# Norm scales of two FFN mixers: two f32r products with a matrix of ones, refined on all partitions, in place of column means and turns

## The chip, the cores and the metric

The kernel runs on one core of a Trainium2 chip. TensorE (PE) multiplies out of SBUF into PSUM, VectorE (DVE), ScalarE (ACT) and GpSimd (POOL) work elementwise, and SP, ACT and POOL issue the DMAs. The metric is the device time of one execution in microseconds, the median of several runs.

## The reference

Two layers of a decoder on 1,024 tokens of 1,024 features. Each layer is a token mixer (layer 0 a gated short convolution, layer 1 banded attention) and a SwiGLU channel mixer with 2,816 hidden features, all with a norm ahead and a residual behind. What is computed at the place of the change is the norm ahead of each channel mixer:

```python
def rmsnorm(x, gain):
    r = lax.rsqrt(jnp.mean(x * x, axis=-1, keepdims=True) + EPS)   # one number for each token
    return (x * r) * gain

x = x + mix                              # mix ends in a product: ... @ w_out (or w_o)
h = rmsnorm(x, norm_ffn[i])
x = x + (silu(g) * u) @ w_down           # g, u = halves of h @ w_gate_up
```

## The kernel before

**Layout.** Activations lie transposed: features on partitions, tokens along a row. `X[m]` (m from 0 to 7) holds 128 features of all 1,024 tokens in f32. Products are made at f32 precision out of f32r parts: every operand is split into a high part (ACT casts it, L881) and a low part (DVE subtracts, L882), and a product is three steps of PE, high by high, high by low, low by high (L1061 to L1063 in the token mixer's output product, L946 to L948 elsewhere), each of 128x128 weights by 512 tokens.

**Order.** Nothing is scheduled by a tool there. A `Line` keeps a time axis in planned microseconds: `line.work` appends work of PE and moves `line.end` on by 0.2265 for each product; `at(t, f)` puts an instruction of another engine at a planned time. Run in order of time, this gives the order in which each engine gets its instructions; an engine then works them in that order, and waits where one is not ready. The planned times are no waits themselves.

**The place.** `channel_mixer` runs once for each layer. First come the eight output tiles of the token mixer's last product for tokens 0 to 511 (half 0), then eight for the other half; `begin1` and `begin2` are the planned ends of the two halves. Behind each tile DVE adds it to the residual (L1087), ACT squares it (L1085), DVE adds the squares (L1091) and POOL stores the residual (L1089). So `state["ss", h]` holds, on 128 partitions, partial sums of squares of each token; what is missing is the sum over partitions, and the result is wanted on all partitions, since `scale` (L1126) multiplies `X[m]` by it in place.

`half_chain(h, t)` makes it, once for each half of each layer, so four times in the kernel. `mean` puts four products on PE, 128 tokens of sums as weights and a column of ones as the moving operand (L1104), which turn the tokens onto partitions: 128x4 sums in PSUM bank P3. These products are f32 and not f32r, and each appears in the trace as two passes. `guess` forms the mean on DVE (L1109) and the inverse root: Ln and Exp on ACT (L263, L264) and one step of Newton on DVE (L265 to L268), all of 128x4. `turn` brings the result back with four transposes of a column that is broadcast to 128 columns (L1116): 128x512 scales in bank P2, equal on all partitions.

**What follows.** The gate-up product is made in one level of Strassen's scheme: seven kinds of products, k = 0 to 6, for four units first, 48 steps of PE for each kind, straight behind `begin2`. Its moving operands are sums of quarters of the scaled X: kind 0 and 1 use half 0 alone (even and odd tiles); kind 2 uses a sum T2 of all four quarters (L1190, L1196), made in four pieces, p = 0 to 3, each split by `put`; kinds 3 to 6 use more such sums (L1200, L1204). So half 0's scales are wanted 192 steps after half 0's last tile, and half 1's 96 steps after its own.

In layer 0 (`whole`) the weight sums for the first four units are also formed in the stretch of half 1's output products (`sums_in_place`, L874), stored to HBM by POOL (L877), and read back later.

Of the kernel before, what the change touches and what calls it, by code (L numbers as in the profile page):

```python
# [44 lines left out]
C_ROOM = 496  # L45
# [25 lines left out]
def trunk_kernel(ctx: ExitStack, tc: tile.TileContext, xT, small, table, w_in, w_out, w_kv, w_q, w_o, w_gu, w_dn, out):  # L71
# [146 lines left out]
    cst = slot("cst", (P, C_ROOM))[:, 0:C_END]  # L218
# [70 lines left out]
    def token_r_rows():  # L289

        ss = state["ss"]
        one = slot("s0", (P, P), F32R)
        dve.memset(plain(one), 1.0)
        hi, lo = slot("G3", dtype=F32R), slot("G4", dtype=F32R)
        m, t, rb = slot("G2"), slot("G5"), slot("G0")
        for h in range(2):
            c = slice(h * 512, h * 512 + 512)
            act.copy(hi[:, c], ss[:, c])
            dve.tensor_tensor(lo[:, c], ss[:, c], plain(hi)[:, c], ALU.subtract)
            ps = bank(("P2", "P3")[h])  # L300
            pe.matmul(ps, one, hi[:, c], start=True, stop=False)
            pe.matmul(ps, one, lo[:, c], start=False, stop=True)
            dve.tensor_scalar(m[:, c], ps, 1.0 / D, EPS, ALU.mult, ALU.add)
            act.activation(t[:, c], m[:, c], AF.Ln)
            act.activation(rb[:, c], t[:, c], AF.Exp, scale=-0.5)
            dve.tensor_tensor(t[:, c], rb[:, c], rb[:, c], ALU.mult)
            dve.scalar_tensor_tensor(t[:, c], t[:, c], -0.5, m[:, c], ALU.mult, ALU.mult)
            dve.scalar_tensor_tensor(rb[:, c], t[:, c], 1.5, rb[:, c], ALU.add, ALU.mult)
        return rb
# [17 lines left out]
    def conv_layer():  # L327
# [33 lines left out]
        for k in range(NK):  # L361
            if 0 < k < NK - 1:
                load_x(k + 1)
                if k % 2:
                    load_parts(k + 1, 2)
            if k == 4:
                nc.sync.dma_start(cst[:, C_SINK:], small[:, C_SINK:])
# [337 lines left out]
        t = group_end  # L705
        back("b0", "G10", t + 40.0)
# [298 lines left out]
    def channel_mixer(layer, next_stage, src_of, operands, raw_tags, extra_tags, slots, line, lead_in):  # L1005
# [12 lines left out]
        def tail_weights(h, m, t):  # L1018
# [18 lines left out]
            if layer == 1:  # L1037
                at(t - 13.0, load_parts)
            else:
                at(t - 14.0, load)  # L1040
                at(t - 5.2, hi)
                at(t - 4.2, lambda: it["steps"][1]())
# [53 lines left out]
        def half_chain(h, t):  # L1096

            v = {}

            def mean():  # L1100
                v["ps"] = bank("P3")
                ss = state["ss", h]
                for b in range(4):
                    pe.matmul(v["ps"][:, b : b + 1], ss[:, b * P : (b + 1) * P], ones, start=True, stop=True)  # L1104

            def guess():
                v["m"] = slot("hr_m", (P, NB, 2), bufs=2)[:, 0:4, 0]
                v["r"] = slot("hr_t", (P, NB, 2), bufs=2)[:, 0:4, 0]
                dve.tensor_scalar(v["m"], v["ps"][:, 0:4], 1.0 / D, EPS, ALU.mult, ALU.add)  # L1109
                rsqrt(v["r"], v["m"], (P, 4))  # L1110

            def turn():
                units["rows", h] = bank("P2")
                for b in range(4):
                    row = v["r"][:, b : b + 1].to_broadcast([P, P])
                    pe.transpose(units["rows", h][:, b * P : (b + 1) * P], row, ident)  # L1116

            at(t + 3.9, mean)
            at(t + 3.95, guess)
            at(t + 5.7, turn)  # L1120

        def scale(h, m):
            c = slice(h * HALF, h * HALF + HALF)
            g0 = C_GAIN + (1 if layer == 0 else 3) * NK
            g = cst[:, g0 + m : g0 + m + 1]
            dve.scalar_tensor_tensor(X[m][:, c], X[m][:, c], g, units["rows", h], ALU.mult, ALU.mult)  # L1126
# [79 lines left out]
        for p in range(4):  # L1206
# [1120 lines left out]
```

## Time and profile before

| | |
|---|---|
| median of 3 runs | 1895.14 us (1894.96 to 1895.24) |
| the profiled execution: its time, and its span | 1894.54 us, 1892.8 us |
| PE busy | 100% of the span, granted clock 1.00 |
| DVE, ACT, POOL busy | 72%, 45%, 17% |
| the four places (start of the column products) | 290.6, 335.5, 1218.2, 1263.2 us |

In the rows of a timeline the columns are the start and the length in us, the engine, the line in the kernel, the operation, the tile written and those read, the shape, and in brackets the engine's idle time just before and what ended it. PEld is PE's loading of weights, which runs beside its products. A group row ends with its count, its busy time and the mean length of one in ns; a row of one line's instructions gives shortest, median and longest in ns.

### The profile page before, as it was taken

The page shows a single profiled execution, that of the slowest core. Times are in us where ns is not written, and L with a number is a line of the kernel's source. Part 1 is how long each engine was busy: PE and PEld are TensorE (multiplying, and loading weights), DVE is VectorE, ACT ScalarE, POOL GpSimd, SP SyncE. Part 2 cuts the span into 40 slices and gives each one's busy share as a digit, 9 for nine tenths or more (in the row PEclk, how much of TensorE's full clock was granted, in tenths as well). Part 3 has the DMA queues.
Part 4 walks back from the last instruction along what each step waited for, and adds up shares of the span by engine and source line. Part 5 has one row for each costly group of instructions (what it writes and reads, how often), then busy time and mean ns, then how long its engine had stood idle before and what let it go on. Part 6 is the DMA issues. An engine that isn't in the chain of part 4 may idle for free.

```text
span 1892.8 us, 24868 instructions
## 1 busy us (share of the span) xinstructions
PE 1887.4 (100%) x8603; PEld 1569.8 (83%) x8603; DVE 1368.5 (72%) x2224; ACT 844.4 (45%) x1694; POOL 319.1 (17%) x620
## 2 busy tenths in 40 slices
PE   9999999999999999999999999999999999999999
PEld 7888888888888888888888888888888888888887
DVE  8997878868778776666678888567767676765543
ACT  6544444533333334444557776335333333344441
POOL 0000011012122221000015777300111111100000
PEclk9999999999999999999999999999999999999999
DMA  8522176146766656987641115844454654577563
GB/s 315 173 96 78 67 292 219 56 162 225 229 215 219 230 200 237 361 295 249 228 138 30 35 25 170 326 147 145 149 179 160 218 183 156 175 279 263 196 226 102
DMA packets 162558, 352.43 MB, mean 186 GB/s; under 512 B 16192, under 2 KB 62656, under 8 KB 162304
## 3 DMA queue, kind: packets, MB, share of 16 engines
q1 hardware_dynamic: 135936, 257.88, 40.8%
q0 software_dynamic: 26208, 92.81, 13.5%
q8 instruction: 67, 1.10, 0.2%
q14 instruction: 59, 0.48, 0.1%
q10 hardware_dynamic: 288, 0.16, 0.0%
HBM read 241.34 MB, written 103.28 MB: 182 GB/s over the span
## 4 chain that ended last, share of the span: by engine, by line
PE 98%; DVE 1%; issue 0%; DMA 0%; ACT 0%; POOL 0%; DVEq 0%; ACTq 0%
PE acc L946 16%; PE acc L948 16%; PE acc L947 16%; PE P L946 9%; PE P L948 9%; PE P L947 9%; PE P L1654 2%; PE P L1656 2%; PE P L1655 2%; PE acc L1061 2%; PE acc L1062 2%; PE acc L1063 2%; PE twin L1881 2%; PE acc L175 1%; PE acc L1961 1%; PE acc L1930 1%
## 5 line engine op out<-in xcount | busy, mean ns | idle before, releaser
L946 PE MATMUL acc<-XS,G 128*128 128x512 f32 x880 | 342.9, 390 | 0.0
L948 PE MATMUL acc<-XS,G 128*128 128x512 f32 x880 | 342.8, 390 | 0.0
L947 PE MATMUL acc<-XS,G 128*128 128x512 f32 x880 | 342.7, 389 | 0.0
L947 PEld LDWEIGHTS acc<-XS,G 128*128 128x128 f32 x880 | 165.3, 188 | 34.2
L946 PEld LDWEIGHTS acc<-XS,G 128*128 128x128 f32 x880 | 165.3, 188 | 34.2
L948 PEld LDWEIGHTS acc<-XS,G 128*128 128x128 f32 x880 | 165.3, 188 | 34.1
L948 PE MATMUL P<-A,G 128*128 128x512 f32 x476 | 185.4, 389 | 0.0
L946 PE MATMUL P<-A,G 128*128 128x512 f32 x476 | 185.4, 389 | 0.0
L947 PE MATMUL P<-A,G 128*128 128x512 f32 x476 | 185.4, 389 | 0.0
L946 PE MATMUL acc<-A,G 128*128 128x512 f32 x441 | 171.8, 390 | 0.0
L948 PE MATMUL acc<-A,G 128*128 128x512 f32 x441 | 171.6, 389 | 0.0
L947 PE MATMUL acc<-A,G 128*128 128x512 f32 x441 | 171.5, 389 | 0.0
L882 DVE TENSOR_TENSOR G<-WL,G 128x512 fp32r<-128x512 f32 x168 | 117.0, 697 | 47.8 <-ACT G L881 47.8
L881 ACT CAST G<-WR 128x512 fp32r<-128x512 f32 (+1 forms) x200 | 120.8, 605 | 59.9 <-PE acc L948 25.9
L882 DVE TENSOR_TENSOR G<-WR,G 128x512 fp32r<-128x512 f32 (+1 forms) x200 | 133.2, 666 | 9.0 <-ACT G L881 8.6
L881 ACT CAST G<-WH 128x512 fp32r<-128x512 f32 (+1 forms) x158 | 95.0, 601 | 83.0 <-PE acc L948 34.0
L1233 ACT ACTIVATE G<-G 128x512 f32<-128x512 f32 x88 | 55.8, 634 | 159.7 <-DVE G L1304 155.6
L946 PE MATMUL P<-XS,G 128*128 128x512 f32 x316 | 123.2, 390 | 0.1
L947 PE MATMUL P<-XS,G 128*128 128x512 f32 x316 | 123.1, 389 | 0.0
L948 PE MATMUL P<-XS,G 128*128 128x512 f32 x316 | 123.1, 389 | 0.0
L881 ACT CAST G<-WL 128x512 fp32r<-128x512 f32 x168 | 103.6, 617 | 42.5 <-DVE WL L821 38.0
L882 DVE TENSOR_TENSOR G<-WH,G 128x512 fp32r<-128x512 f32 (+1 forms) x158 | 106.6, 675 | 7.9 <-ACT G L881 7.7
(332 smaller groups left out, 3801.4 us busy)
## 6 DMA issues: line engine op xcount, KB each, us to landing
G<-h SPq DMA_DIRECT2D x70, 512.0 KB, 5.1
h<-X POOLq DMA_DIRECT2D x44, 512.0 KB, 5.3
X<-in_w_dn SPq DMA_DIRECT2D x80, 256.0 KB, 3.7
s<-X POOLq DMA_DIRECT2D x40, 512.0 KB, 4.5
WR<-in_w_gu SPq DMA_DIRECT2D x36, 512.0 KB, 5.7
WH<-in_w_gu SPq DMA_DIRECT2D x36, 512.0 KB, 6.2
h<-X POOLq DMA_DIRECT2D x66, 256.0 KB, 3.6
WR<-s SPq DMA_DIRECT2D x54, 256.0 KB, 3.4
```

What stands on the lines that cost most here:

```text
L881: lambda: act.copy(out_hi, raw),
L882: lambda: lo_eng.tensor_tensor(out_lo, raw, plain(out_hi), ALU.subtract),
L946: pe.matmul(ps[:, q], w[:, 0, c], x[:, 0, q], start=start and e == 0, stop=False, skip_group_check=True)
L947: pe.matmul(ps[:, q], w[:, 0, c], x[:, 1, q], start=False, stop=False, skip_group_check=True)
L948: pe.matmul(ps[:, q], w[:, 1, c], x[:, 0, q], start=False, stop=last, skip_group_check=True)
L1061: pe.matmul(ps, hi[:, kc], xs[:, 0, c], start=k == 0, stop=False, skip_group_check=True)
L1062: pe.matmul(ps, hi[:, kc], xs[:, 1, c], start=False, stop=False, skip_group_check=True)
L1063: pe.matmul(ps, lo[:, kc], xs[:, 0, c], start=False, stop=k == n_op - 1, skip_group_check=True)
L1233: state["silu"] = act.activation(x, x, AF.Silu)
L1654: pe.matmul(ps, x[:, 0, t], hi, start=k == 0, stop=False)
L1655: pe.matmul(ps, x[:, 0, t], lo, start=False, stop=False)
L1656: pe.matmul(ps, x[:, 1, t], hi, start=False, stop=k == NK - 1)
```

## The change

`half_chain` no longer turns anything. ACT casts the 128x512 sums of squares to f32r (into G10), DVE subtracts for the low part, and PE multiplies both by a constant 128x128 matrix that holds 1/1024 everywhere, adding up in P3. The mean of each token then stands on all partitions at once. ACT takes Ln (adding EPS from a column of constants) and Exp into P2, and the square into G11; DVE makes the step of Newton in two instructions on 128x512. That step leaves the result with a factor of -2, which is taken up by a second copy of the gains, times -0.5. Planned times around it are moved to fit. A function that no one called is dropped.

```diff
+    def rms_constants():
+        dve.memset(plain(means), 1.0 / D)
+        dve.memset(cst[:, C_EPS : C_EPS + 1], EPS)
+        for i, stage in enumerate((1, 3)):
+            g = cst[:, C_GAIN + stage * NK : C_GAIN + (stage + 1) * NK]
+            dve.tensor_scalar(cst[:, C_HALF + i * NK : C_HALF + (i + 1) * NK], g, -0.5, None, ALU.mult)
...
+        def hi():
+            v["x"] = parts()
+            act.copy(v["x"][:, 0], ss())
+        def lo():
+            dve.tensor_tensor(v["x"][:, 1], ss(), plain(v["x"])[:, 0], ALU.subtract)
+        def sums():
+            v["m"] = mean()
+            for e in (0, 1):
+                pe.matmul(v["m"], means, v["x"][:, e], start=e == 0, stop=e == 1)
+        def guess():
+            y = v["y"] = rows()
+            act.activation(y, v["m"], AF.Ln, bias=cst[:, C_EPS : C_EPS + 1])
+            act.activation(y, y, AF.Exp, scale=-0.5)
+            v["q"] = square()
+            act.activation(v["q"], y, AF.Square)
+        def newton():
+            dve.scalar_tensor_tensor(v["q"], v["m"], EPS, v["q"], ALU.add, ALU.mult)
+            dve.scalar_tensor_tensor(v["y"], v["q"], -3.0, v["y"], ALU.add, ALU.mult)
...
         t = group_end
+        at(t + 45.0, rms_constants)
...
                 at(t - 5.2, hi)
-                at(t - 4.2, lambda: it["steps"][1]())
+                at(t - 4.6, lambda: it["steps"][1]())
...
-            at(t + 3.9, mean)
-            at(t + 3.95, guess)
-            at(t + 5.7, turn)
+            for d, f in zip((2.3, 2.9, 3.7, 3.75, 5.9), steps):
+                at(t + d, f)
...
-                ts = (t + 8.0, t + 10.0, t + 18.0)
-                at(t + 12.0, sums_in_place, pairs[u], 0)
-                at(t + (15.2 if u == 3 else 14.0), sums_in_place, pairs[u], 2)
-                at(t + (16.7 if u == 3 else 15.5), store_sums, pairs[u], first_sums[layer][u])
+                d = (0.0, 0.0, 3.0, 4.0)[u]
+                ts = (t + 8.0, t + 10.0, t + 18.0 + 1.5 * d)
+                at(t + 12.0 + d, sums_in_place, pairs[u], 0)
+                at(t + 14.0 + 1.5 * d, sums_in_place, pairs[u], 2)
+                at(t + 15.5 + 1.5 * d, store_sums, pairs[u], first_sums[layer][u])
...
-        pace = 1.2 if tail > 3.5 else 1.1
-        t = begin1 + 6.2
+        pace = (1.2, 1.8)[whole]
+        t = begin1 + 7.6
         for odd in (0, 1):
             if odd and whole:
-                t = begin1 + 28.0
+                pace, t = 1.2, begin1 + 31.0
...
-        t = begin2 + 6.2
+        t = begin2 + 7.0
...
             put(2, p, lambda p=p: T2[p // 2][:, p % 2], t + 2.4)
-            t += 3.2
+            t += 2.4
...
             put(3, p, lambda p=p: X[2 * p][:, hi_half], t + 0.6)
-            t += 2.2
+            t += 2.4
```

How the rows move, at three places. In the rows stand the line (the kernel's lines are shifted by 13 to 23 in the changed one: L1087 is L1110, L1126 is L1138, L882 is L905), the operation, the tile written and those read with buffer numbers behind their names, and the shape. PE in layer 0, behind half 0, before:

```order
L1063 MATMUL acc0_363_2455<-A5_305_2064,WL_360_2425 128x512
L1104 MATMUL P3_369_2488<-cst_2_64,s0_322_2184 128x1 x4
L1061 MATMUL acc0_363_2455<-XS4_310_2083,WH_359_2424 128x512
...
L1063 MATMUL acc1_373_2509<-A0_290_1959,WL_365_2461 128x512
L1116 MATMUL P2_376_2517<-cst_2_64,hr_t_371_2494 128x128 x4
L1061 MATMUL acc1_373_2509<-A1_292_1967,WH_364_2460 128x512
```

and now:

```order
L1086 MATMUL acc0_364_2460<-A5_306_2069,WL_361_2430 128x512
L318 MATMUL P3_371_2496<-G10_369_2485,means_3_65 128x512 x2
L1084 MATMUL acc0_364_2460<-XS4_311_2088,WH_360_2429 128x512
L1085 MATMUL acc0_364_2460<-XS4_311_2088,WH_360_2429 128x512
L1086 MATMUL acc0_364_2460<-XS4_311_2088,WL_361_2430 128x512
```

The two products stand where the column products stood; nothing stands in place of the turns, nine products further on. The same holds at the other three places.

DVE at the same place (s0 are the sums of squares, WL the low part of an output weight), before:

```order
L1087 TENSOR_TENSOR X7_350_2350<-acc3_358_2419,X7_350_2350 128x512
L882 TENSOR_TENSOR WL_365_2461<-WR_357_2405,WH_364_2460 128x1024
L1091 TENSOR_TENSOR s0_322_2184<-s0_322_2184,G11_366_2466 128x512
L1109 TENSOR_SCALAR hr_m_370_2493<-P3_369_2488 128x4
L265 TENSOR_TENSOR rs_t_372_2496<-hr_t_371_2494 128x4
```

and now:

```order
L1110 TENSOR_TENSOR X7_351_2355<-acc3_359_2424,X7_351_2355 128x512
L905 TENSOR_TENSOR WL_366_2466<-WR_358_2410,WH_365_2465 128x1024
L1114 TENSOR_TENSOR s0_323_2189<-s0_323_2189,G11_367_2471 128x512
L313 TENSOR_TENSOR G10_369_2485<-s0_323_2189,G10_369_2485 128x512
L1110 TENSOR_TENSOR X0_299_2028<-acc0_364_2460,X0_299_2028 128x512
L328 SCALAR_TENSOR_TENSOR G11_373_2502<-P3_371_2496,G11_373_2502 128x512
L329 SCALAR_TENSOR_TENSOR P2_372_2499<-G11_373_2502,P2_372_2499 128x512
```

The weight split still stands between the last residual add and the last add of squares; the subtract of the new chain is put behind these, and the next tile's residual add ahead of the step of Newton.

DVE in layer 1, at the end of operand 2 (XS1 takes the last two pieces' low parts, L1190 and L1196 make the sum T2, G tiles are low parts of weights), before:

```order
L1126 SCALAR_TENSOR_TENSOR X7_1565_10791<-X7_1565_10791,cst_2_64,P2_1644_11422 128x512
L1190 TENSOR_TENSOR X6_1564_10789<-X6_1564_10789 128x512
L1196 TENSOR_TENSOR WL_1659_11507<-X7_1565_10791,X6_1564_10789 128x512
L882 TENSOR_TENSOR G1_1662_11527<-WH_1652_11463,G1_1662_11527 128x512
L1271 TENSOR_TENSOR G10_1648_11447<-P3_1661_11521,G10_1648_11447 128x512
L882 TENSOR_TENSOR XS1_1650_11450<-WL_1659_11507,XS1_1650_11450 128x512
```

and now:

```order
L905 TENSOR_TENSOR XS1_1648_11432<-WL_1655_11477,XS1_1648_11432 128x512
L1203 TENSOR_TENSOR X6_1563_10780<-X6_1563_10780 128x512
L1209 TENSOR_TENSOR WL_1655_11477<-X7_1564_10782,X6_1563_10780 128x512
L1284 TENSOR_TENSOR G9_1641_11400<-P1_1654_11473,G9_1641_11400 128x512
L905 TENSOR_TENSOR XS1_1648_11432<-WL_1655_11477,XS1_1648_11432 128x512
```

Two instructions that stood ahead of the last low part, G1's and the add into G10, now stand behind it: from the first scaling up to and with that low part DVE has 25 instructions, where it had 27. In layer 0 it has 22 where it had 23.

More of the change, by code (lines that the diff above doesn't have):

```diff
@@ L44 @@
 C_END = C_OWN + P
-C_ROOM = 496
+C_HALF = C_END
+C_EPS = C_HALF + 2 * NK
+C_ROOM = 368
 WARM = 8
@@ L215, in times @@
             dve.tensor_tensor(out_t[:, c], src, in1[:, c], ALU.mult)
-    cst = slot("cst", (P, C_ROOM))[:, 0:C_END]
+    cst = slot("cst", (P, C_ROOM))
+    means = slot("means", (P, P), F32R)
     nc.scalar.dma_start(cst[:, :C_SINK], small[:, :C_SINK])
@@ L287, in token_mean @@
         dve.tensor_scalar(m, ps[:, 0:4], 1.0 / D, EPS, ALU.mult, ALU.add)
[L289 to L309, printed above, removed]
+    def rms_constants():
[4 more added lines that the diff above has]
+            dve.tensor_scalar(cst[:, C_HALF + i * NK : C_HALF + (i + 1) * NK], g, -0.5, None, ALU.mult)
@@ new lines, in half_gain, with rms_rows @@
+    def half_gain(i, m):
+        return cst[:, C_HALF + i * NK + m : C_HALF + i * NK + m + 1]
+    def rms_rows(ss, parts, mean, rows, square):
+        v = {}
+        def hi():
[16 more added lines that the diff above has]
+            dve.scalar_tensor_tensor(v["y"], v["q"], -3.0, v["y"], ALU.add, ALU.mult)
+        return hi, lo, sums, guess, newton
@@ L366, in conv_layer @@
             if k == 4:
-                nc.sync.dma_start(cst[:, C_SINK:], small[:, C_SINK:])
+                nc.sync.dma_start(cst[:, C_SINK:C_END], small[:, C_SINK:])
             if k < 2 or k % 2 == 0:
@@ L1096, in half_chain, with rows @@
         def half_chain(h, t):
[L1098 to L1112, printed above, removed]
-                units["rows", h] = bank("P2")
-                for b in range(4):
-                    row = v["r"][:, b : b + 1].to_broadcast([P, P])
-                    pe.transpose(units["rows", h][:, b * P : (b + 1) * P], row, ident)
-            at(t + 3.9, mean)
-            at(t + 3.95, guess)
-            at(t + 5.7, turn)
+            def rows():
+                units["rows", h] = bank("P2")
+                return units["rows", h]
+            steps = rms_rows(
+                lambda: state["ss", h],
+                lambda: slot("G10", (P, 2, HALF), F32R),
+                lambda: bank("P3"),
+                rows,
+                lambda: slot("G11", (P, HALF)),
+            )
+            for d, f in zip((2.3, 2.9, 3.7, 3.75, 5.9), steps):
+                at(t + d, f)
         def scale(h, m):
             c = slice(h * HALF, h * HALF + HALF)
-            g0 = C_GAIN + (1 if layer == 0 else 3) * NK
-            g = cst[:, g0 + m : g0 + m + 1]
+            g = half_gain(layer, m)
             dve.scalar_tensor_tensor(X[m][:, c], X[m][:, c], g, units["rows", h], ALU.mult, ALU.mult)
```

## The prediction

> **What bounds the kernel now.** I read first the page's first two lines and the chain of work that ended last, then the waits of TensorE, then the stretches around the changed lines.
>
> ```profile
> span 1892.8 us, 24868 instructions
> PE 1887.4 (100%) x8603; PEld 1569.8 (83%) x8603; DVE 1368.5 (72%) x2224; ACT 844.4 (45%) x1694; POOL 319.1 (17%) x620
> ...
> PE 98%; DVE 1%; issue 0%; DMA 0%; ACT 0%; POOL 0%; DVEq 0%; ACTq 0%
> ...
> PE P L353 <- DVE s L350: 1.1, 1, 1.1
> PE acc L1930 <- POOL G L1924: 0.2, 1, 0.2
> ```
>
> The last two rows are all waits listed for PE: 1.3 us. PE's stream of products is the kernel's length, so a microsecond off that stream is one off the end, and whatever the other engines gain or lose counts only if it makes a product wait. So the question is what the stream pays at the four places (two halves in two layers). The first, the columns being start, length, engine, line:
>
> ```profile
> 285.82 0.39 PE L1061 MATMUL acc<-XS,WH 128*128 128x512 f32 x1
> ...
> 290.36 0.39 PE L1063 MATMUL acc<-A,WL 128*128 128x512 f32 x1
> 290.58 0.95 PE L1104 MATMUL P<-cst,s 128*128 128x1 f32 x8
> 291.39 0.49 PE L1061 MATMUL acc<-XS,WH 128*128 128x512 f32 x1
> 291.72 0.40 PE L1062 MATMUL acc<-XS,WH 128*128 128x512 f32 x1
> ...
> 293.57 0.60 PE L1116 MATMUL P<-cst,hr_t 128*128 128x128 f32 x4
> 293.93 0.48 PE L1061 MATMUL acc<-A,WH 128*128 128x512 f32 x1
> ...
> 296.08 0.39 PE L1061 MATMUL acc<-A,WH 128*128 128x512 f32 x1
> ...
> 1262.95 0.39 PE L948 MATMUL acc<-A,G 128*128 128x512 f32 x1
> 1263.18 0.95 PE L1104 MATMUL P<-cst,s 128*128 128x1 f32 x8
> ...
> 1268.68 0.39 PE L946 MATMUL acc<-A,G 128*128 128x512 f32 x1
> ```
>
> Read starts, not lengths: a product is shown 0.39 long, but the next starts 0.227 later (20 steps from 285.82 to 290.36). From 290.36 to 296.08 there are 19 steps of ordinary products. At 0.227 they need 4.31; they took 5.72. So the column products (L1104) and turns (L1116) cost the stream **1.41** at this place. The last two marks say the same of the fourth: 19 steps, 5.73 us.
>
> **The change part by part.** *Removed from PE*: at each place 1.41 us. *Added to PE*: two products of 512 columns, by the steady step 2 x 0.227 = 0.45. Net per place 0.96, over four places **3.84 us**, if nothing waits.
>
> *Added elsewhere*, for each place: ACT a cast, Ln, Exp and Square of 128x512 (before: Ln and Exp of 128x4); DVE a subtract and two scalar-tensor-tensor of 128x512 (before: five of 128x4). Sums of squares to operands is now a longer chain, and both its ends touch PE.
>
> *End one: the products need the split of the sums of squares.* Layer 0, first half, by the timeline (WL is the low part of a weight of the output product):
>
> ```profile
> 286.52 1.05 ACT L881 CAST WH<-WR 128x1024 fp32r<-128x1024 f32 x1 [3.09 <-PE acc L1062]
> 287.48 0.63 ACT L1085 ACTIVATE G<-X 128x512 f32<-128x512 f32 x1
> 287.61 1.23 DVE L882 TENSOR_TENSOR WL<-WR,WH 128x1024 fp32r<-128x1024 f32 x1 [0.21 <-ACT WH L881]
> 288.75 0.69 DVE L1091 TENSOR_TENSOR s<-s,G 128x512 f32<-128x512 f32 x1
> ...
> L881 ACT CAST G<-WL x168: 602/622/626, 119.5 to 1669.2; 128x512 fp32r<-128x512 f32 x168
> ```
>
> The last square was ready at 288.11, but its add stood behind a weight split and ended at 289.44; the change leaves that order. Then the cast of 0.62 and the subtract of 0.69, each 0.04 after what it waits for (the split above began at 287.61 and its cast ended at 287.57): low part at 290.87 with its signal. PE reads it in the second product, whose weight load would start at 290.58, with the first product. 0.29 late. What lateness costs is shown by the one such wait there is:
>
> ```profile
> 79.18 0.39 PE L948 MATMUL P<-XS,G 128*128 128x512 f32 x1
> ...
> 79.65 0.19 PEld L946 LDWEIGHTS P<-XS,G 128*128 128x128 f32 x1 [0.51 <-ACT G L614]
> ...
> 79.99 0.40 PE L947 MATMUL P<-XS,G 128*128 128x512 f32 x1
> ```
>
> The wait stands at the weight load: due at 79.18, it began at 79.65, 0.47 late, and the second product after 79.18 came at 79.99 in place of 79.63: 0.36 lost. So cost is lateness less 0.11, here **0.18** (bounds 0.1 and 0.3). Queued behind it on PE is everything; on DVE, behind the subtract, the residual add of the next output tile, not needed for microseconds. At the other three places the add is not behind a split and ends 1.7 us ahead of the products, as here in layer 1, second half: 1261.44 against 1263.18; cast and subtract fit in that.
>
> ```profile
> 1260.75 0.69 DVE L1091 TENSOR_TENSOR s<-s,G 128x512 f32<-128x512 f32 x1 [0.76 <-ACT G L1085]
> ...
> 1266.81 1.41 DVE L1126 SCALAR_TENSOR_TENSOR X<-X,cst,P 128x512 f32<-128x512 f32 x2 [1.21 <-PE P L1116]
> ...
> 1283.53 0.68 DVE L882 TENSOR_TENSOR XS<-WL,XS 128x512 fp32r<-128x512 f32 x1
> ...
> 1284.32 0.19 PEld L947 LDWEIGHTS acc<-XS,G 128*128 128x128 f32 x1
> ```
>
> *End two: the third kind's operands.* These rows are the tightest spot near the change. After the scale rows, DVE makes four pieces of operand 2; the low part of the last ends at 1284.21 and its weight load starts at 1284.32: 0.11 of slack. I count from the start of the mean products (1263.18): first scaling at 3.63, load due at 21.14. After the change the load is due 0.96 earlier: 20.18. The first scaling comes later. Rows for its links:
>
> ```profile
> L1267 ACT COPY G<-acc x44: 580/587/590, 334.4 to 1657.8; 128x512 f32<-128x512 f32 x44
> ...
> L1079 ACT ACTIVATE s<-X x3: 631/631/632, 254.1 to 1221.5; 128x512 f32<-128x512 f32 x3
> ...
> L525 ACT ACTIVATE X<-G,cst x16: 711/725/727, 121.9 to 228.5; 128x512 f32<-128x512 f32 x16
> ...
> L1126 DVE SCALAR_TENSOR_TENSOR X<-X,cst,P x32: 734/740/748, 294.2 to 1280.3; 128x512 f32<-128x512 f32 x32
> ```
>
> Second product ends 0.23 + 0.39 = 0.62; Ln 0.69 (a copy out of PSUM, 0.59, and 0.1 for an operand out of a column: 0.73 against 0.63 in the rows); Exp 0.59; Square 0.60; two DVE steps of 0.69; six handovers of 0.04. Sum 4.12. No row here has ACT writing 512 columns to PSUM, so the bounds are three times 0.587 with 0.685 for DVE (3.99) and three times 0.725 with 0.74 (4.51); I take 4.12, nearest to the copy. Against it, the shorter spacing takes two instructions out of DVE's way: 27 stood from first scaling to that last low part, 25 do now. 26 steps from 1266.81 to 1283.53 are 0.643 each; 24 of them, 15.43, and 0.1 because only one instruction is left between the last sum and its low part to cover ACT's cast. Low part ends at 4.12 + 15.53 + 0.69 = 20.34, its signal 20.38, due 20.18: 0.20 late, cost about **0.15** (by the two bounds 0 and 0.5). In layer 0 the same piece was ready at 354.56 and due at 356.67:
>
> ```profile
> 353.87 0.69 DVE L882 TENSOR_TENSOR XS<-WL,XS 128x512 fp32r<-128x512 f32 x1
> ...
> 356.67 0.19 PEld L947 LDWEIGHTS acc<-XS,XS 128*128 128x128 f32 x1
> ```
>
> Of these 2.11 it loses 0.49, 0.96 and 0.1, and one instruction fewer in its way gives 0.64 back: 1.2 are left, cost 0.
>
> Operand 4 comes off the same DVE queue:
>
> ```profile
> 1292.57 0.69 DVE L882 TENSOR_TENSOR G<-WH,G 128x512 fp32r<-128x512 f32 x1 [1.21 <-ACT G L881]
> ...
> 1304.71 0.69 DVE L882 TENSOR_TENSOR XS<-X,XS 128x512 fp32r<-128x512 f32 x1
> ...
> 1306.08 0.19 PEld L947 LDWEIGHTS acc<-XS,G 128*128 128x128 f32 x1
> ```
>
> Slack 0.68; it loses 0.49 (later start) and 0.81 (earlier due, less the wait above), and regains most of the 1.21 wait of the first row, since ACT's cast for that weight now stands ahead of the operand's. About 0.1 left: cost **0**, up to 0.5 if that order doesn't help.
>
> *Moved at no cost*: the wider spacing in layer 0's first half and the later weight sums lie under 43 us of output products; POOL's store of a pair of sums goes out behind one residual store more, and its reader belongs to the fourth kind of product, after all of these. The constants are four small DVE instructions in the first mixer. The earlier low split of output weights leaves DVE's order at the place unchanged.
>
> Sum: 3.84 - 0.18 - 0.15 = 3.5. The profiled execution took 1894.54 (span 1892.8), 0.6 under the median of the runs; 1894.54 - 3.5 = 1891.0, and on the median **1891.6 us**.
>
> The page "ScalarE: Activation LUTs" of the Trainium skill ("Step-by-step") says that ScalarE writes PSUM faster than SBUF. No run here shows it for 512 columns; if it takes 0.04 off Ln and Exp each, the wait in layer 1 shrinks by 0.08 and the sum would be 1891.5. The page "TensorE: Matmul & The Clock Gate" (the table of specs at its head) says that TensorE's queue pulls weight loads ahead of products in flight. By that rule alone both waits would be a step shorter and the sum 1891.4; the load held at 79.65 speaks against it, since its product and the one behind it came late with it.
>
> **Rivals.** *No waits* (both ends just in time): 3.84, 1891.3. For it: 0.2 and 0.3 are a few handovers; against it: the split ahead of the add is in the rows. *The chain decides in layer 1*: with the upper bounds 0.3 + 0.5 + 0.5 are lost, 2.5 gained, 1892.6. For it: 0.11 of slack before; against it: nothing but the bounds. *Slower than before*: ACT and DVE on P2 and P3 run far beyond their rows while PE writes other banks. Each us of chain costs one in layer 1, and in layer 0 from 1.2 on; the gain is gone at 2.3 us more, that is five links 1.7 times as long as their rows; at 3 us more 0.2 + 3.1 + 1.8 = 5.1 is lost, 1896.4. L1126 reads P2 under running products at 0.74, which speaks against it. *The change doesn't do what it says*: products with ones cost as much as what they replace; with the first wait 1895.3. Against: the ordinary products change their weights at each step and keep 0.227.
>
> **How the numbers follow.** Forecast 0.55, no waits 0.22, chain in layer 1 0.18, slower 0.02, no effect 0.03. The range must leave out no more than 0.2: from 1891.0 (no waits, and 0.3 for what the rows round) to 1892.8. About 0.2%, 3.8 us, is what a measurement of this kernel can tell: the border is 1891.35, just above the case of no waits. Most of that case (0.16) and a little of the forecast (0.08) fall under it: faster 0.24; slower by as much needs over 7.6 us of waits: 0.02; the rest, 0.74, is within.
>
> **What would show it.** Nineteen ordinary steps and the two new products, 4.76 us from 0.23 ahead of them, at three places, and at the first 0.1 to 0.3 more, with PE's load waiting for the subtract. A wait of PE for DVE at operand 2 in layer 1, of 0.05 to 0.3, and none in layer 0. First scaling about 4.1 after the products start. It is wrong if products with ones take over 0.23, if Ln or Exp into PSUM differ from 0.59 to 0.73, or if PE waits anywhere else.

## The result, and the profile after

| | before | changed |
|---|---|---|
| median of 15 runs each | 1894.96 us (1894.41 to 1895.78) | 1891.11 us (1890.71 to 1891.63) |
| the profiled execution: time, span | 1894.54 us, 1892.8 us | 1890.71 us, 1889.0 us |

The ratio is 0.9980, with a 95% interval of 0.9973 to 0.9986: 3.85 us less. The interval leaves out no change, and the ratio lies at the border of 0.2% that the prediction set. One execution in the experiments below ran at a granted clock of 0.65 and took 2712.82 us; it enters no figure.

First the head of the changed kernel's page, then its waits by who waited for whom (total us, times, longest), for PE and for its weight loads:

```profile
span 1889.0 us, 24784 instructions
PE 1883.7 (100%) x8563; PEld 1565.0 (83%) x8563; DVE 1373.1 (73%) x2220; ACT 851.4 (45%) x1702; POOL 320.6 (17%) x620
...
PE P L375 <- DVE s L372: 1.1, 1, 1.1
PE acc L1943 <- POOL G L1937: 0.2, 1, 0.2
...
PEld P L318 <- DVE G L313: 0.3, 1, 0.3
PEld acc L970 <- DVE XS L905: 0.2, 1, 0.2
```

PE's own list is what it was, 1.3 us that have nothing to do with the change. The two new waits stand only in the list of its weight loads: L318, a product with ones, waiting for the low part of the sums of squares, and L970, operand 2, waiting for its low part. Those are the two that the prediction named.

The starts of the four places and of the last product, on PE's timeline:

```profile
290.36 0.78 PE L318 MATMUL P<-G,means 128*128 128x512 f32 x2
...
334.53 0.62 PE L318 MATMUL P<-G,means 128*128 128x512 f32 x2
...
1216.26 0.62 PE L318 MATMUL P<-G,means 128*128 128x512 f32 x2
...
1260.24 0.62 PE L318 MATMUL P<-G,means 128*128 128x512 f32 x2
...
1884.93 0.28 PE L971 MATMUL acc<-A,G 128*128 128x256 f32 x1
```

and the same marks of the kernel before that the prediction did not show:

```profile
335.52 0.28 PE L1104 MATMUL P<-cst,s 128*128 128x1 f32 x2
...
1218.24 0.28 PE L1104 MATMUL P<-cst,A 128*128 128x1 f32 x2
...
1888.75 0.28 PE L948 MATMUL acc<-A,G 128*128 128x256 f32 x1
```

Differences of these starts give the ledger, each stretch beginning with the place that it is named by (taken from starts in ns, so some differ by 0.01 from the rounded rows):

| stretch of PE's stream | before | changed | gained |
|---|---|---|---|
| up to the first place | 290.58 | 290.36 | 0.22 |
| place 1 (layer 0, half 0) to place 2 | 44.94 | 44.17 | 0.77 |
| place 2 to place 3 | 882.72 | 881.73 | 0.99 |
| place 3 to place 4 | 44.94 | 43.97 | 0.97 |
| place 4 (layer 1, half 1) to the last product | 625.57 | 624.70 | 0.87 |

From the first place on that is 3.60 us: 0.97 and 0.99 at two places, 0.2 less at the first, 0.1 less at the fourth. The 0.22 ahead of the first place is not the change's, as further executions show below.

The first place and its wait, by the timeline of the changed kernel:

```profile
287.39 1.23 DVE L905 TENSOR_TENSOR WL<-WR,WH 128x1024 fp32r<-128x1024 f32 x1 [0.21 <-ACT WH L904]
288.53 0.69 DVE L1114 TENSOR_TENSOR s<-s,G 128x512 f32<-128x512 f32 x1
289.25 0.62 ACT L310 CAST G<-s 128x512 fp32r<-128x512 f32 x1 [1.36 <-DVE s L1114]
289.90 0.69 DVE L313 TENSOR_TENSOR G<-s,G 128x512 fp32r<-128x512 f32 x1 [0.69 <-ACT G L310]
290.65 0.19 PEld L318 LDWEIGHTS P<-G,means 128*128 128x128 f32 x1 [0.32 <-DVE G L313]
```

The weight split (L905) stands ahead of the last add of squares, the cast and the subtract follow, and the load that was due at 290.36 begins at 290.65: 0.29 late.

The fourth place, and the end of operand 2 behind it:

```profile
1260.89 0.66 ACT L322 ACTIVATE P<-P,cst 128x512 f32<-128x512 f32 x1 [1.23 <-PE P L318]
1261.58 0.58 ACT L323 ACTIVATE P<-P 128x512 f32<-128x512 f32 x1
1262.20 0.60 ACT L325 ACTIVATE G<-P 128x512 f32<-128x512 f32 x1
1262.83 0.69 DVE L328 SCALAR_TENSOR_TENSOR G<-P,G 128x512 f32<-128x512 f32 x1 [2.95 <-ACT G L325]
1263.56 0.70 DVE L329 SCALAR_TENSOR_TENSOR P<-G,P 128x512 f32<-128x512 f32 x1
1264.29 1.41 DVE L1138 SCALAR_TENSOR_TENSOR X<-X,cst,P 128x512 f32<-128x512 f32 x2
...
1279.85 0.69 DVE L905 TENSOR_TENSOR XS<-WL,XS 128x512 fp32r<-128x512 f32 x1
1280.60 0.19 PEld L970 LDWEIGHTS acc<-XS,G 128*128 128x128 f32 x1 [0.23 <-DVE XS L905]
1280.63 0.46 PE L970 MATMUL acc<-XS,G 128*128 128x512 f32 x1
1280.93 0.40 PE L971 MATMUL acc<-XS,G 128*128 128x512 f32 x1
```

The chain runs without a gap: first scaling 4.05 us behind the start of the products (1264.29 - 1260.24). The load of the last low part was due at 20.18 from there, 1280.42, and began at 1280.60: 0.18 late. (A load is due when the product ahead of its own starts. The 0.23 in the brackets is longer, since it counts from the end of the load before.) The product behind it starts 0.30 later in place of 0.227, so 0.07 is lost.

### The profile page after: what moved, and what is told of

The parts are those of the page before. It is cut to its first block, busy times and chain, and to the rows that moved or that the text cites. A ratio compares the mean times of both kernels' runs of the same rounds, so it can differ in the third digit from the quotient of the medians.

```text
span 1889.0 us, 24784 instructions
## 1 busy us (share of the span) xinstructions
PE 1883.7 (100%) x8563; PEld 1565.0 (83%) x8563; DVE 1373.1 (73%) x2220; ACT 851.4 (45%) x1702; POOL 320.6 (17%) x620
## 4 chain that ended last, share of the span: by engine, by line
PE 98%; DVE 1%; issue 0%; ACT 0%; POOL 0%; DMA 0%; DVEq 0%; ACTq 0%
PE acc L969 16%; PE acc L971 16%; PE acc L970 16%; PE P L969 9%; PE P L971 9%; PE P L970 9%; PE P L1667 2%; PE P L1669 2%; PE P L1668 2%; PE acc L1085 2%; PE acc L1086 2%; PE acc L1084 2%; PE twin L1894 2%; PE acc L177 1%; PE acc L1974 1%; PE acc L1943 1%
## 5 line engine op out<-in xcount | busy, mean ns | idle before, releaser
L970 PE MATMUL acc<-XS,G 128*128 128x512 f32 x880 | 342.4, 389 | 0.0
L970 PEld LDWEIGHTS acc<-XS,G 128*128 128x128 f32 x880 | 165.2, 188 | 34.6 <-DVE XS L905 0.2
L970 PE MATMUL P<-A,G 128*128 128x512 f32 x476 | 185.2, 389 | 0.0
L970 PE MATMUL acc<-A,G 128*128 128x512 f32 x441 | 171.3, 389 | 0.0
L905 DVE TENSOR_TENSOR G<-WL,G 128x512 fp32r<-128x512 f32 x168 | 117.1, 698 | 49.0 <-ACT G L904 49.0
L905 DVE TENSOR_TENSOR G<-WR,G 128x512 fp32r<-128x512 f32 (+1 forms) x200 | 134.4, 672 | 9.5 <-ACT G L904 9.1
L970 PE MATMUL P<-XS,G 128*128 128x512 f32 x316 | 122.9, 389 | 0.0
L905 DVE TENSOR_TENSOR G<-WH,G 128x512 fp32r<-128x512 f32 (+1 forms) x158 | 106.7, 675 | 4.2 <-ACT G L904 4.2
```

Source lines behind the costliest of these rows:

```text
L905: lambda: lo_eng.tensor_tensor(out_lo, raw, plain(out_hi), ALU.subtract),
L970: pe.matmul(ps[:, q], w[:, 0, c], x[:, 1, q], start=False, stop=False, skip_group_check=True)
```

## The experiments

All were timed against runs of the kernel before on the same chip. Single executions of one kernel scatter by 1 us and more, and the three medians of before lie between 1894.96 and 1895.23, so for the small terms I read each kernel's trace from its first place to its last product, where the same kernel repeats to some hundredths unless the text says otherwise.

**Both waits taken out.** One weight split goes behind the chain's subtract in layer 0; in layer 1 one low part of a weight goes behind operand 2's last piece.

```diff
-                at(t - 4.6, lambda: it["steps"][1]())
+                at(t - (2.4 if (h, m) == (1, 1) else 4.6), lambda: it["steps"][1]())
...
-            at(t + 0.8, lambda: it["steps"][1]())
+            at(t + 0.8 + lag, lambda: it["steps"][1]())
...
-                    ring_granule(4, ops_of, 0, get, start, True, src=src)
+                    ring_granule(4, ops_of, 0, get, start, True, src=src, lag=2.6 if layer and (k, u) == (2, 2) else 0.0)
```

> The changed kernel (1891.11) with two DVE instructions put later: in layer 0 the low part of the weight that stood ahead of the last add of squares (now behind the chain's subtract), and in layer 1 one low part of a weight that stood ahead of operand 2's last piece (now behind it). Theory: the changed kernel loses 0.18 us at the first place (second ones-product's weight load 0.29 late) and 0.07 us at operand 2 in layer 1 (load 0.19 late), and nothing else at the four places. Both waits go: each place costs 0.453 us beyond ordinary steps, total 1891.11 - 0.25 = 1890.9. Rival, waits are slack (PE makes them up, as nothing of 0.25 shows in the median gain of 3.85 against 3.84 without waits): 1891.1, and the trace shows the same time between the place and a mark behind it. Rival, a next wait close behind (operand 4 in layer 1 has 0.12 of slack): a part of the 0.07 comes back there, 1891.0.

Measured: 1891.14 (1890.75 to 1891.45) against 1895.12 for before, ratio 0.9978 (0.9969 to 0.9987). In the trace both waits are gone: the sums' low part is done at 290.65, ahead of both loads (the first at 290.80), and operand 2's low part ends 0.47 ahead of its load:

```profile
289.96 0.69 DVE L313 TENSOR_TENSOR G<-s,G 128x512 fp32r<-128x512 f32 x1 [0.69 <-ACT G L310]
290.57 1.22 DVE L905 TENSOR_TENSOR WL<-WR,WH 128x1024 fp32r<-128x1024 f32 x1
290.80 0.41 PEld L318 LDWEIGHTS P<-G,means 128*128 128x128 f32 x2
...
1279.77 0.69 DVE L905 TENSOR_TENSOR XS<-WL,XS 128x512 fp32r<-128x512 f32 x1
1280.93 0.19 PEld L970 LDWEIGHTS acc<-XS,G 128*128 128x128 f32 x1
```

The stretch from place 1 to place 2 fell by 0.19 (44.17 to 43.97, rounded), that behind place 4 by 0.06 (624.70 to 624.64). At the first place 0.17 of the wait's cost stands in the two steps at the late load, and 0.02 in the next few, which in the changed kernel take 0.231 to 0.236 in place of 0.227. At operand 2 the same count gives 0.07 and 0.02, 0.09, so 0.03 of it came back: operand 4's low part was done at 1302.65, its load began 0.01 behind its due time, and six steps from 1302.69 on took 0.03 more together. So the first rival, that PE makes waits up, is refuted by the trace, and the second, a next wait close behind, was right for a third of operand 2's wait. Over the whole the trace gained 0.19 and not 0.25, since the stretch from place 2 to place 3 took 0.06 longer, at a wait near 425 us (below). The times can't tell: against its own runs of before the kernel gains 3.98, the changed one 3.85, and the two intervals overlap.

**The old spacing of operand 2's pieces.** 3.2 planned us in place of 2.4, all else as changed.

```diff
-            t += 2.4
+            t += 3.2
```

> The changed kernel with the four pieces of operand 2 planned 3.2 us apart, as before, in place of 2.4. Theory: only the order on DVE counts; with 3.2 two instructions more (0.6 each) stand ahead of the last low part in layer 1. Load 0.19 + 1.2 = 1.4 late, 1.3 lost there in place of 0.07; layer 0 had 1.64 of slack, keeps about 1.0, loses nothing. 1891.11 + 1.2 = 1892.3. Rival, the planned times are no waits and the spacing is cosmetic: 1891.1. Rival, the one instruction more that then lies between the last sum and its low part covers ACT's cast and the loss is 0.1 less: 1892.2.

Measured: 1892.45 (1892.12 to 1892.94), ratio 0.9985 (0.9976 to 0.9993). The trace from the first place on is 1.09 longer than the changed kernel's, all but 0.02 of it at operand 2 in layer 1, where first its high part and then its low part is waited for:

```profile
1281.63 0.19 PEld L969 LDWEIGHTS acc<-XS,G 128*128 128x128 f32 x1 [0.79 <-ACT XS L904]
1282.36 0.19 PEld L970 LDWEIGHTS acc<-XS,G 128*128 128x128 f32 x1 [0.54 <-DVE XS L905]
```

1.14 is lost there in place of 0.07; I had expected 1.3, or 0.1 less with the cast covered. So the tighter spacing, a line of the diff that looks like tidying, carries 1.1 of the gain: without it the change is worth about 2.5 by the trace (2.67 by the times).

**Layer 1 as before.** The column products, turns and planned times of before in layer 1 (the spacing of operand 2's pieces too), the new ones in layer 0.

```diff
         def half_chain(h, t):
+            if layer == 1:
+                return old_chain(h, t)
...
-        t = begin2 + 7.0
+        t = begin2 + (7.0 if whole else 6.2)
```

> Layer 0 as changed, layer 1 with the column products, turns and planned times of before. Theory: places 1 and 2 give 0.97 each less 0.18 of wait, 1.75 in all; places 3 and 4 cost 1.42 as before and operand 2 in layer 1 is just in time as before. Against before (1894.96): 1893.2. Rival, a part of the gain of 3.85 comes from elsewhere in the program (the profiled run of the changed kernel is 0.22 ahead already at the first place): 1893.0 and the same 0.2 at the first place here too. Rival, most of the gain is in one layer: 1892.3 or 1893.9.

Measured: 1893.41 (1892.97 to 1895.14) against 1895.12, 1.71 gained where 1.75 was expected; but the ratio is 0.9992 (0.9983 to 1.0001), so the times alone don't show a gain. A further execution gave the trace:

> Layer 0 as changed, layer 1 as before once more, for the trace. Theory: from the first place to the end PE needs 1598.17 us in the kernel before and 1594.57 in the changed one; here 1598.17 - 1.75 = 1596.4, with 0.62 at place 1 (0.45 and 0.17 of wait), 0.45 at place 2, 1.42 at places 3 and 4, and no wait at operand 2 in layer 1. Rival, gain outside the places: less than 1596.2.

From first place to last product 1596.46, as expected 1596.4. Place 1 again had the late load (0.29 and 0.34 between starts in place of two steps of 0.227), places 3 and 4 the old products and turns at the old price, and operand 2 in layer 1 no wait. Of the 3.60 layer 0 gives 1.70 here, so layer 1 gives the other 1.9: the gain lies in both layers, at the places.

**Longer chains.** Copies in place between Exp and Square, four in layer 0's half 1 and one in layer 1's; they change no value.

```diff
             act.activation(y, y, AF.Exp, scale=-0.5)
+            for _ in range(extra):
+                act.copy(y, y)
...
+                (0, 4 if layer == 0 else 1)[h],
```

> The changed kernel with ACT copies of 128x512 inside the chain of half 1, result unchanged: four of them in layer 0, one in layer 1, 0.58 + 0.03 each. Theory: in layer 1 the chain is what operand 2 waits for, so one copy adds its whole length: load 0.19 + 0.61 = 0.80 late, 0.7 lost in place of 0.07. In layer 0 operand 2 has 1.64 of slack (low part done at 353.03, load at 354.71): four copies, 2.44, make it 0.8 late, 0.7 lost. Together 1891.11 + 0.6 + 0.7 = 1892.4. Rival, the wait at operand 2 belongs to DVE's amount of work and not to the chain: DVE was idle 2.95 us ahead of its first step, and a later start is made up: 1891.1 to 1891.5. Rival, no slack in layer 0 either: 1894.

Measured: 1893.03 (1892.71 to 1893.84), ratio 0.9989 (0.9980 to 0.9997), 0.6 more than expected; by the trace from the first place on 1.69 more than the changed kernel, where 1.3 was expected. What waited (the first row is the four copies):

```profile
336.81 2.38 ACT L325 COPY P<-P 128x512 f32<-128x512 f32 x4
...
350.04 0.39 PE L973 MATMUL P<-XS,G 128*128 128x512 f32 x1
...
350.45 0.68 DVE L1287 TENSOR_TENSOR G<-P,G 128x512 f32<-128x512 f32 x1
351.18 0.19 PEld L971 LDWEIGHTS P<-XS,G 128*128 128x128 f32 x1 [1.18 <-DVE G L1287]
...
1277.37 0.19 PEld L971 LDWEIGHTS P<-A,G 128*128 128x128 f32 x1 [0.58 <-DVE G L1287]
...
1282.60 0.19 PEld L972 LDWEIGHTS acc<-XS,G 128*128 128x128 f32 x1 [0.37 <-DVE XS L907]
```

The length of the chain does reach PE, but not first at operand 2. The second kind's last unit needs a PSUM bank that an add on DVE (L1287 here, L1284 in the changed kernel) frees, and that add stands behind the scalings. In the changed kernel's layer 0 the bank has 1.26 of slack (its load due 15.19 behind the place, at 349.72; the add over at 348.41 and its signal 0.05 later), operand 2 has 1.64, so the bank decides. The copies put the add off by 2.40: the load was due at 350.04, with the product ahead of it, and began at 351.18, 2.40 - 1.26 = 1.14 late (the bracket's 1.18 is the time since the load before), and 1.03 was lost. In layer 1 one copy cost 0.43 at the bank and 0.22 at operand 2, 0.65 together, where 0.7 was expected for operand 2 alone: the bank's slack there was only some 0.06.

**High part alone.** The last add of squares writes f32r itself; the cast, the subtract and the low part's product are left out, and the one product stands six steps earlier.

```diff
-            for e in (0, 1):
-                pe.matmul(v["m"], means, v["x"][:, e], start=e == 0, stop=e == 1)
+            pe.matmul(v["m"], means, parts()[:, 0], start=True, stop=True)
...
+                if m == NK - 1:
+                    units["parts", h] = slot("G10", (P, 2, HALF), F32R)
+                    to = units["parts", h][:, 0]
+                dve.tensor_tensor(to, state["ss", h], units["sq", h, m], ALU.add)
...
-            for d, f in zip((2.3, 2.9, 3.7, 3.75, 5.9), steps):
+            for d, f in zip((2.4, 2.45, 4.6), steps[2:]):
```

> One ones-product in place of two: the last add of squares writes f32r itself, ACT's cast, DVE's subtract and the product of the low part are left out (so the sums of squares enter the mean rounded to f32r), and the product stands six steps earlier; the weight's low part in layer 0 stands behind that add, as in the first experiment. Theory, PE's stream is the time: each place costs 0.227 beyond ordinary steps, 0.907 less in all; both waits (0.17 and 0.07) go, since the chain starts 1.36 earlier. 1891.1 - 1.15 = 1889.95. Rival, a wait takes the place of the removed ones (the load of the sums, since the add of squares ends only some 0.4 ahead of the earlier product, or ACT's copies of the first units, which now stand behind the chain): 1890.3 or more.

Measured: 1889.98 (1889.80 to 1890.40), ratio 0.9973 (0.9962 to 0.9983), the fastest kernel of this study: 5.25 under before on its chip, where the changed kernel had 3.85. In the trace no load waits at a place or at operand 2:

```profile
288.29 0.69 DVE L1117 TENSOR_TENSOR G<-s,G 128x512 fp32r<-128x512 f32 x1 [0.75 <-ACT G L1107]
288.90 1.22 DVE L904 TENSOR_TENSOR WL<-WR,WH 128x1024 fp32r<-128x1024 f32 x1
289.14 0.19 PEld L317 LDWEIGHTS P<-G,means 128*128 128x128 f32 x1
289.37 0.39 PE L317 MATMUL P<-G,means 128*128 128x512 f32 x1
```

From the first place to the end, less the six steps by which the place stands earlier, 1593.39: 1.18 less than the changed kernel, where 1.15 was expected. Each product with ones is worth one step, and with the chain shorter, and the weight's split behind the add, both waits are gone. The price is precision: sums of squares rounded to f32r go into the mean.

**One f32 product.** The matrix of ones and the sums in f32, no split.

```diff
-            for e in (0, 1):
-                pe.matmul(v["m"], means, v["x"][:, e], start=e == 0, stop=e == 1)
+            pe.matmul(v["m"], plain(means), ss(), start=True, stop=True)
```

> One f32 product of 128x512 with the matrix of ones, straight from the f32 sums: no cast, no subtract, no low part; six steps earlier, the weight's low part in layer 0 behind the add. Theory: an f32 product is two passes (the four column products of before show eight records of 0.111), and for 512 columns a pass moves at half the columns per us at best, so it costs four ordinary steps, 0.907, where the pair of f32r products costs 0.453. Four places: 1.81 more, 0.24 of waits less: 1891.1 + 1.6 = 1892.7. Rival, two passes at the ordinary step: 0.453 as now, and the waits gone: 1890.9. Rival, f32 is dearer still, eight steps: 1896.3.

Measured: 1892.91 (1892.58 to 1893.68), ratio 0.9987 (0.9978 to 0.9996). On PE's timeline:

```profile
289.82 1.02 PE L317 MATMUL P<-s,means 128*128 128x512 f32 x2
290.28 0.80 PE L1083 MATMUL acc<-A,WH 128*128 128x512 f32 x1
290.92 0.40 PE L1084 MATMUL acc<-A,WH 128*128 128x512 f32 x1
291.15 0.40 PE L1085 MATMUL acc<-A,WL 128*128 128x512 f32 x1
```

The start of the second ordinary product behind it (L1085) is 1.33 from the f32 product's; two steps of 0.227 off, it cost 0.88, 3.9 ordinary steps, against 0.45 for the pair that it replaces. Expected were 0.907 and 1892.7. The page "FP8 and Floating Point Precision" of the Trainium skill ("TensorE Precision Notes") counts four passes through the array for true f32; the 3.9 steps agree. Splitting into two f32r parts is worth 0.42 of PE for each place, as long as the cast and the subtract find room beside it.

**Scales in SBUF.** The rows in the tile of the sums of squares and not in PSUM, at three of the four places.

```diff
-                units["rows", h] = bank("P2")
-                return units["rows", h]
+                units["rows", h] = bank("P2") if layer and h == 0 else state["ss", h]
+                return units["rows", h]
```

> The scales lie in SBUF (in the tile of the sums of squares) in place of PSUM bank P2, at three of the four places (not layer 1, half 0). In the changed kernel's trace the scaling (L1138), which reads P2, is followed 0.66 later by the next DVE instruction, one that reads SBUF alone 0.60 later. Theory: of the eight scalings of layer 1's half 1 each gives 0.06, 0.48 in all, and ACT loses some 0.1 where Exp and Square read and Ln and Exp write SBUF (casts from SBUF to SBUF take 0.62, Exp in PSUM 0.58): operand 2's low part comes 0.38 earlier, the 0.19 wait of its load is gone, 0.07 gained: 1891.04; no difference to be told in the time, but in the trace. Rival, PSUM costs nothing and the 0.66 belongs to the form (a column of gains): scalings stay at 0.66, the wait stays or grows to 0.3.

Measured: 1891.52 (1891.16 to 1892.17), ratio 0.9981 (0.9972 to 0.9989). The kernel has both forms, so its groups show them side by side (shortest, median, longest in ns):

```profile
L322 ACT ACTIVATE s<-P,cst x3: 689/690/690, 291.7 to 1261.4; 128x512 f32<-128x512 f32 x3
L322 ACT ACTIVATE P<-P,cst x1: 662/662/662, 1217.4 to 1217.4; 128x512 f32<-128x512 f32 x1
L323 ACT ACTIVATE s<-s x3: 633/633/633, 292.4 to 1262.1; 128x512 f32<-128x512 f32 x3
L323 ACT ACTIVATE P<-P x1: 582/582/582, 1218.1 to 1218.1; 128x512 f32<-128x512 f32 x1
...
L1138 DVE SCALAR_TENSOR_TENSOR X<-X,cst,s x24: 741/744/752, 296.2 to 1276.6; 128x512 f32<-128x512 f32 x24
L1138 DVE SCALAR_TENSOR_TENSOR X<-X,cst,P x8: 736/740/748, 1220.9 to 1238.6; 128x512 f32<-128x512 f32 x8
```

My theory fell. DVE's scaling takes 0.740 out of PSUM and 0.744 out of SBUF: the 0.06 over its other instructions belongs to its form. ACT is slower in SBUF, by 0.028 for Ln (written there) and 0.051 for Exp (read and written there). Operand 2's load was then 0.30 late and cost 0.19, which is the rival's figure. What the prediction cited from the page "ScalarE: Activation LUTs" of the Trainium skill ("Step-by-step"), that ScalarE writes PSUM faster than SBUF, is borne out by 0.028 a write.

**Three more executions of unchanged kernels.** Twice the kernel before, once the changed one.

> The kernel before once more, for a second trace. The timed gain of the changed kernel and of the experiments against the runs of before beside them is 0.15 to 0.45 more than their traces give from the first place to the end (3.85 against 3.60; 5.25 against 4.78). Theory: the first profiled execution of before was one of its fast ones (1894.54, medians 1894.96 to 1895.23), and other executions lose 0.2 to 0.5 more, either ahead of the first place (first column product at 290.6 there; the ones-product at 290.4 to 291.0 in the others) or near 425 in layer 0, where DVE waits 4.7 to 5.5 us for a DMA of hidden rows and PE loses up to 0.5 from about 4.9 on. Then the four places cost 1.42 each here too, and the stretch from the first place to the end is 1598.17 plus what is lost near 425. Rival: the places themselves cost more in other executions, 1.5 or more each.

> The changed kernel once more, for a second trace. Theory: 0.62 at place 1, 0.45 at the others, 0.07 at operand 2 in layer 1, so 1594.57 from the first place to the end, plus what is lost near 425 if the DMA there lands late (DVE waiting over 4.9 us); and the first place at 290.4 to 291.0. Rival: the two waits vary by more than 0.05 from execution to execution.

> The kernel before a third time, as in the look before: places 1.42 each, first place between 290.4 and 291.0, and a loss near 425 only where DVE waits over 4.9 us for the DMA.

Measured: 1895.07, 1891.61, 1895.83. The stretches from place 1 to 2, from 3 to 4 and from 4 to the end repeat to 0.01: 44.94, 44.94 and 625.57 in both of before, 44.16, 43.97 and 624.70 in the changed one. The rival (places that cost more in other executions) is refuted, and so is a varying wait. Three other things vary. The first place stood at 290.8, 290.9 and, beyond what was expected, 291.2; over the nine traces with the new chain it lies between 290.4 and 291.2 (where the place stands six steps earlier, these are added), and over three of before between 290.6 and 291.2, so the 0.22 of the first pair was chance. In all three, made on one chip, the products between about 1040 and 1185 us stand further apart than in the nine other traces: from 1055 to 1185 the mean of the steps of 0.2 to 0.3 us is 228.8 to 228.9 ns against 228.2 to 228.3, and over the stretch this is 0.3 us, which the expectations did not have. And near 425 us in layer 0 DVE waits for a DMA of hidden rows, 4.78 us in the first profiled execution of before, 4.75 in the second, and in the third:

```profile
421.31 0.69 DVE L1315 TENSOR_TENSOR X<-X 128x512 f32<-128x512 f32 x1 [5.38 <-DMA h<-X]
...
428.92 0.19 PEld L946 LDWEIGHTS P<-A,G 128*128 128x128 f32 x1 [0.50 <-DVE s L1278]
```

Counted as what PE's steps behind it take beyond 0.227, waits up to 4.81 cost nothing, 4.87 and 4.88 cost 0.02 and 0.04 (high part alone, longer chains), 5.03 cost 0.07 (both waits out), 5.38 cost 0.41, and 5.53 cost 0.58 (one f32 product).

## Why the prediction was right, point by point

*What bounds the kernel.* Right. Every difference found, in the change and in seven other kernels, is one of PE's stream.

*Removed and added on PE: 0.96 for each place, 3.84.* Right: 0.97 and 0.99 at the places without a wait, 0.97 at the first with its wait taken out.

*End one, the first place.* Right in place, cause and size: 0.29 late as forecast, 0.17 lost in the two steps at the load where 0.18 was forecast by the rule "lateness less 0.11", read from the stall at 79.18; with the slower steps behind it the wait cost 0.19. That rule held again at operand 2 (0.18 late, 0.07 lost; 0.30 and 0.19 with the scales in SBUF) and in the longer chain of layer 0 (1.14 late, 1.03 lost). It does not count the 0.02 to 0.03 in the steps behind. The prediction's sentence on the rule of the Trainium skill's page "TensorE: Matmul & The Clock Gate" (the table of specs at its head), by which both waits would be a step shorter, is not borne out: what PE saves of a late load is half a step, 0.11.

*End two, operand 2.* The links came out at 0.66, 0.58, 0.60, 0.69 and 0.70 where 0.69, 0.59, 0.60, 0.69 and 0.69 were summed; first scaling at 4.05 for 4.12; load 0.18 late for 0.20. The cost is the term that was mis-sized: "cost about 0.15" did not use the rule of the paragraph above it, which gives 0.09; 0.07 was measured in the two steps, 0.09 with those behind. That two instructions fewer in DVE's way buy 1.2 us is what the old spacing showed (1.07 more lost).

*Layer 0, operand 2: "1.2 are left, cost 0".* The cost was right and the slack wrong: 1.64 by the rows

```profile
352.34 0.69 DVE L905 TENSOR_TENSOR XS<-WL,XS 128x512 fp32r<-128x512 f32 x1
...
354.71 0.19 PEld L970 LDWEIGHTS acc<-XS,XS 128*128 128x128 f32 x1
```

The first scaling came 0.07 sooner than summed. From it to the end of the low part DVE took 14.45 (338.58 to 353.03), where it had taken 15.40 before (339.15 to 354.56): 0.95 less, where one instruction fewer was put at 0.64 and 0.1 of waiting was added. And not this operand but the PSUM bank of the second kind is the first to be late. The prediction did not have the bank, so its sentence that each us of chain costs in layer 0 only from 1.2 on names the wrong reader; in layer 1 the bank was 0.06 from costing something. *Operand 4: about 0.1 left*: right, low part done at 1302.13, load at 1302.27; with PE 0.09 earlier it began to cost, as the first experiment showed.

*The sum.* 3.84 - 0.18 - 0.15 = 3.5; the traces give 3.60 from the first place on, and the corrected sum is 3.84 - 0.19 - 0.09 = 3.56. The timed difference of 3.85 is a quarter of a us more than the traces give. With 1891.11 the time falls nearer to the rival "no waits" (1891.3) than to the forecast (1891.6), yet the traces show both waits. Part of that is where the forecast started: from a median of before of 1895.14, which was 1894.96 in the runs of the result, 0.18 less. Five of the other kernels with the new chain in both layers (the sixth's profiled execution lost 0.58 near 425) also gained 0.16 to 0.5 more by their times than by their traces, set against the first trace of before, whose 1894.54 was among its fastest executions. Where a typical execution of before loses that much is not shown: the DMA near 425 cost 0.41 in one of its three traces, but also 0.07 and 0.58 in two of the nine with the new chain. This stays open.

*The other rivals.* Products with ones as dear as what they replace, and slow ACT or DVE on PSUM banks, are refuted by the step of 0.227 and by the links above. Of the signs of being wrong that the prediction named, one came out by a hair: Exp took 0.58, just below its 0.59 to 0.73; Ln at 0.66 and the products stayed inside, and PE waited nowhere else.

## What to carry to other kernels

A sum over partitions that is wanted on all partitions costs two ordinary steps of PE as f32r parts against a matrix of ones, and one step if the high part will do; column products and turns, small as they are, cost six (1.41 us): the trace shows twelve passes there, whose starts are some 0.11 us apart, with 1 column as with 128. When such a chain moves work from PE to ACT and DVE, list every load and every bank that PE takes from behind it with its slack, because the order of DVE's queue then decides how much of the gain is left: here a spacing of planned times was worth 1.1 us of 3.6. And terms of a tenth of a us are read between marks in the trace, since whole times also hold the chance of start-up and of DMAs.

## What the runs showed that I had not expected

DVE reads a scale from PSUM as fast as from SBUF in a scalar-tensor-tensor of 128x512 (0.740 and 0.744). The page "Perfetto Trace Analysis" of the Trainium skill ("Optimizing Scalar/DVE Operations") gives DVE about twice the fixed cost on PSUM (125 against 60 ns); no such difference appears here with one of two inputs in PSUM.

Between 1055 and 1185 us all three traces of one chip show steps 0.6 ns longer in the mean than the nine other traces, with the granted clock at 1.00 in both and equal steps (226.7 ns) between 800 and 940 us; what sets it no run tells.
